# The MoE norm's gain moved from the rows into the experts' weight splits, and the second half's routing put ahead of weight splits on VectorE

## The chip, the cores and the metric

One core of one Trainium2 chip runs the kernel. The metric is the device time of one execution in microseconds (us). The core has five engines that work side by side: TensorE (PE, matmuls), VectorE (DVE), ScalarE (ACT), GpSimd (POOL) and SyncE (SP), of which the last issues most of the DMA transfers and POOL issues the gathers and scatters by index.

## The reference

One hybrid decoder layer on 1024 tokens of width 1024, in float32. Ahead of the part that is changed, a convolution branch, a forgetting attention and a cross-attention into 256 memory tokens are added to x. Then comes the mixture of experts, in two levels: the best of 4 groups, and of its 4 experts the best two.

```python
x = x + hierarchical_moe(rmsnorm(x, norm_moe_g[l]), ...)
return rmsnorm(x, norm_final_g)

def rmsnorm(x, g):
    y = xf * lax.rsqrt(jnp.mean(xf * xf, axis=-1, keepdims=True) + EPS)
    return y * g

def hierarchical_moe(h, wg, bg, we, be, w_gate, w_up, w_down):
    g_logits = hf @ wg + bg
    g_star = argmax(softmax(g_logits))
    e_sel = (hf @ we + be) of group g_star
    top_v, top_i = lax.top_k(softmax(e_sel), 2)
    weights = p_gsel[:, None] * top_v / sum(top_v)
    a = hf @ w_gate[e];  b = hf @ w_up[e]
    y = sum over e of (silu(a) * b * combine[e]) @ w_down[e]
```

Each of 16 experts has w_gate and w_up of 1024x256 and w_down of 256x1024.

## The kernel before

Every float32 product is made of three matmuls. An operand is split into a high part, rounded to the format that PE multiplies, and a low part, what is left of it: `split` writes the high part on ScalarE (line L134) and the low part on VectorE (L138) or GpSimd (L136). PE then multiplies high by high, low by high and high by low (L142 to L144). Weights come from memory as raw tiles (`w_raw` for the layers ahead, `e_raw` for gate and up, `d_raw` for down), 128x1024 at a time, and are split on the way. The split results are called `w_hi`, `w_lo`, `gu` and `dn`, and those of token rows `xgT`.

The tokens go through the end of the layer in two halves of 512 (four tiles of 128 rows). `xa_out(n)` adds the cross-attention of half n to x, makes the sums of squares and the router's raw products. `rows_of(hf)` turns the sums into the inverse root of the norm (n3v, n3t, n3r: some twelve small VectorE operations, with three Newton steps), scales the logits lg by it, writes the normed rows to memory (`h3_dram`), from which the experts' rows are gathered, and hands lg to the routing. The rows of the first half are scaled on ScalarE and multiplied by the gain `grow` on GpSimd (L926, tiles h3s); those of the second half are multiplied by the gain on GpSimd first, ahead of the norm (`gained`, L819, tiles hg), and scaled on ScalarE afterwards (L918). `grow` is the gain spread over all 128 partitions; the gain is also there as `g_moe`, eight columns with one number per partition, for use on transposed data.

`route_steps` finds the best group and the two best experts by masks (m, fm_s, fm_b, oh, ohg, E), counts tokens by matmuls (`M`, place in the queue of an expert, tm, q), builds selection matrices Am and B, and sums them on PE into slots (`slot_sums`, L1081). From these come `ids`, the list of token rows of each expert. It is a generator: its first piece runs to Am, and later pieces make the sums and ids.

`fetch` gathers rows xg by `ids` with a DMA that GpSimd issues (L1305). `turn` transposes them on PE (L1251, into the bank ps_tra) and splits them into xgT. `early_steps` and `early` multiply xgT with gate and up weights (ps_lin) and make uu, the activated product; `store` multiplies with the down weights and adds to the output by index. The first two experts' first-half rows are multiplied early, between the two routings, and fill PE while the second half is routed. Most experts' rows beyond 128 go in a second pass with fewer rows that uses the raw weights without splits (`gate_up_low`, `store_low`); for these `turn` copies the transposed rows with one ScalarE operation (L1316).

A scheduler orders each engine's instructions by the order in the code, which `tc.high_priority(offset)` moves ahead by so many places and `tc.issue_after` holds behind an instruction; the result is one fixed list for each engine, in which each instruction waits for its inputs.

Of the kernel before, what the change touches and what calls it, by code (L numbers as in the profile page):

```python
# [16 lines left out]
P = 128  # L17
D = 1024
T = 1024
KD = 8  # L20
# [35 lines left out]
def half(n):  # L56
    return slice(n * HALF, n * HALF + HALF)
# [7 lines left out]
def layer_kernel(ctx, tc, a, out, dbg=None):  # L65
# [700 lines left out]
    st, HG = {}, {}  # L766

    def xa_out(n):
# [19 lines left out]
        for m in range(KD):  # L788
# [5 lines left out]
            if m == 4:  # L794
                for k in range(4):
                    products(k)
                rows(0)
                if n:
                    HG[0] = gained(0)
# [10 lines left out]
        if n:  # L810
            HG[1] = gained(1)
        return ss

    def gained(b):

        tiles = [xt_p.tile([P, 2, HALF], F32, name=f"hg{b}", tag=("xt1a", "xt1b")[b], bufs=2) for _ in range(2)]
        hg = [x[:, i] for x in tiles for i in range(2)]
        for t in range(4):
            G.tensor_tensor(hg[t], x3[4 + t][:, half(b)], grow[:, half(b)], op=OP.mult)  # L819
        return hg  # L820
# [58 lines left out]
    grow = ro.tile([P, D], F32, name="grow", tag="grow", bufs=1)  # L879
    G.dma_start(grow, bcast_rows(a["moe_g_row"], D))  # L880
# [22 lines left out]
    def rows_of(hf, ss, htile=None):  # L903
# [10 lines left out]
        for i in range(H4):  # L914
            if hf:
                for b in range(2):
                    h = HG[b][i]
                    A.activation(h, h, AF.Copy, scale=r[:, i:i + 1])  # L918
                    nc.sync.dma_start(h3_dram[blk(t0 + i), half(b)], h)
                continue  # L920
            h = htile()
            if i in ():
                V.scalar_tensor_tensor(h, x3[t0 + i], r[:, i:i + 1], grow, op0=OP.mult, op1=OP.mult)
            else:
                A.activation(h, x3[t0 + i], AF.Copy, scale=r[:, i:i + 1])
                G.tensor_tensor(h, h, grow, op=OP.mult)  # L926
            nc.sync.dma_start(h3_dram[blk(t0 + i)], h)
# [266 lines left out]
    def gu_weights(src, tile_, raw_=raw_tile, parts=range(4), raws=None):  # L1194
        gu = [[], [], []]
        for b in parts:
# [6 lines left out]
            split(t[0], t[1], raw)  # L1203
# [24 lines left out]
    with pool("rows") as rw:  # L1228
# [7 lines left out]
        lg0 = rows_of(0, ss0, lambda: rw.tile([P, D], F32, name="h3s", tag="h3s", bufs=2))  # L1236
# [4 lines left out]
        with tc.high_priority(offset=600):  # L1241
            lg1 = rows_of(1, ss1)
# [65 lines left out]
    def turn(e, h):  # L1308
        if is_shared(e) and h == 1:
# [6 lines left out]
            A.activation(XT[e, h], pt, AF.Copy)  # L1316
# [123 lines left out]
    with tc.issue_after(order["mm"].ins):  # L1440
        next(route1)
# [69 lines left out]
    gfin = ro.tile([P, D], F32, name="gfin", tag="grow", bufs=1)  # L1511
# [212 lines left out]
```

## Time and profile before

| what | value |
|---|---|
| median of 3 runs | 1228.31 us (1223.48 to 1232.91) |
| the profiled execution | 1228.64 us |
| its span, first to last instruction | 1226.9 us |
| granted clock of PE, mean | 0.985 of full speed |
| PE busy | 1159.0 us, 94% |
| DVE, ACT, POOL busy | 843.0, 629.3, 404.5 us |

All times of rows count from the start of the span; the profiled execution is 1.7 us longer than its span. [...] A row of a timeline gives the start, the length, the engine, the line and operation, what is written and read, how many instructions of the kind follow one another, and in brackets how long the engine had been idle and what it waited for.

### The profile page before, as it was taken

The numbers are of one execution on the slowest core, as the hardware profiler recorded it, in microseconds if no ns is written. First come the engines' busy times: TensorE is split into PE (matmuls) and PEld (weight loads), VectorE is DVE, ScalarE is ACT, GpSimd is POOL, SyncE is SP. The second block draws the span as 40 slices with busy tenths as digits, with TensorE's granted clock in tenths as the row PEclk, the third lists the DMA queues.
The fourth block names the chain that finished last, engine by engine and source line by source line (L and its number), as shares of the span: only waits on it lengthen the run. The fifth ranks groups of instructions, "written<-read, shape, count | busy, mean of one in ns | idle before, by whom it ended". The sixth has DMA issues, their size and how long they took to land. (4 is left out here: it accounts for less than half of the span.)

```text
span 1226.9 us, 17120 instructions
## 1 busy us (share of the span) xinstructions
PE 1159.0 (94%) x6173; PEld 908.7 (74%) x6174; DVE 843.0 (69%) x1569; ACT 629.3 (51%) x1059; POOL 404.5 (33%) x276
## 2 busy tenths in 40 slices
PE   7999999999999999999999999999977898999995
PEld 3678887878877777788888788788754666667773
DVE  5499998653969787791235754755997784766665
ACT  6345664442646555471333342733742575767765
POOL 3327996221010100101012665273034133233433
PEclk9999999999999999999999999999998898999998
DMA  5211224136111111111343453144356889999967
GB/s 208 75 37 52 58 97 156 51 106 231 53 57 44 44 59 46 39 55 46 103 163 129 155 167 111 66 123 121 101 192 243 270 243 300 301 292 311 320 169 285
DMA packets 57467, 174.12 MB, mean 142 GB/s; under 512 B 7992, under 2 KB 11080, under 8 KB 57376
## 3 DMA queue, kind: packets, MB, share of 16 engines
q1 hardware_dynamic: 49680, 149.76, 36.5%
q0 software_dynamic: 7696, 23.20, 8.1%
q8 instruction: 51, 0.84, 0.3%
q14 instruction: 40, 0.33, 0.1%
HBM read 136.92 MB, written 36.01 MB: 141 GB/s over the span
## 5 line engine op out<-in xcount | busy, mean ns | idle before, releaser
L136 POOL TENSOR_TENSOR w_lo<-w_raw,w_hi 128x1024 fp32r<-128x1024 f32 x58 | 140.1, 2415 | 463.4 <-ACT w_hi L134 453.6
L144 PE MATMUL ps_lin<-hh,w_lo 128*128 128x512 f32 x560 | 221.4, 395 | 2.5 <-POOL w_lo L136 2.5
L142 PE MATMUL ps_lin<-hh,w_hi 128*128 128x512 f32 x560 | 223.0, 398 | 0.7 <-DVE u L357 0.6
L143 PE MATMUL ps_lin<-hl,w_hi 128*128 128x512 f32 x560 | 221.5, 396 | 0.0
L134 ACT ACTIVATE w_hi<-w_raw 128x1024 fp32r<-128x1024 f32 (+1 forms) x100 | 92.1, 921 | 201.0 <-PE ps_lin L143 169.1
L144 PEld LDWEIGHTS ps_lin<-hh,w_lo 128*128 128x128 f32 x560 | 105.3, 188 | 24.6 <-POOL w_lo L136 4.6
L142 PEld LDWEIGHTS ps_lin<-hh,w_hi 128*128 128x128 f32 x560 | 105.4, 188 | 23.3 <-issue 2.9
L143 PEld LDWEIGHTS ps_lin<-hl,w_hi 128*128 128x128 f32 x560 | 105.4, 188 | 21.5 <-issue 1.6
L379 DVE SCALAR_TENSOR_TENSOR ps_cva<-u,dw_w,ps_cva 128x1024 f32<-128x1024 f32 x90 | 111.6, 1280 | 0.5
L138 DVE SCALAR_TENSOR_TENSOR gu<-e_raw,gu 128x1024 fp32r<-128x1024 f32 x64 | 77.5, 1222 | 4.5 <-ACT gu L134 0.8
L375 POOL TENSOR_TENSOR oc<-oc,pj 128x512 f32<-128x512 f32 x60 | 75.8, 1303 | 8.8 <-ACT pj L374 8.7
L134 ACT ACTIVATE gu<-e_raw 128x1024 fp32r<-128x1024 f32 x64 | 67.4, 1058 | 8.0 <-PE ps_lin L144 7.4
L142 PE MATMUL ps_lin<-gu,xgT 128*128 128x512 f32 x144 | 58.8, 408 | 4.1 <-ACT xgT L134 4.1
L374 ACT ACTIVATE pj<-u,dw_w 128x512 f32<-128x512 f32 x60 | 42.4, 721 | 34.3 <-POOL oc L375 34.2
L138 DVE SCALAR_TENSOR_TENSOR dn<-d_raw,dn 128x1024 fp32r<-128x1024 f32 x32 | 39.0, 1225 | 27.8 <-ACT dn L134 24.0
L1305 POOL DMA_INDIRECT xg<-h_dram,ids x29 | 35.2, 1215 | 67.5 <-PE ps_sco L1081 24.3
L143 PE MATMUL ps_lin<-gu,xgT 128*128 128x512 f32 x144 | 57.4, 399 | 0.0
L560 ACT ACTIVATE sc<-sc,mns 128x128 f32<-128x128 f32 (+3 forms) x64 | 49.4, 772 | 15.6 <-DVE mns L556 15.0
L144 PE MATMUL ps_lin<-gu,xgT 128*128 128x512 f32 x144 | 57.0, 396 | 0.0
L138 DVE SCALAR_TENSOR_TENSOR pl<-ps_tra,ph 128x512 fp32r<-128x512 f32 (+1 forms) x80 | 49.1, 636 | 9.3 <-ACT ph L134 8.2
L134 ACT ACTIVATE ph<-ps_tra 128x512 fp32r<-128x512 f32 (+1 forms) x80 | 41.8, 552 | 23.3 <-PE ps_tra L573 22.5
L573 PE MATMUL ps_tra<-ident,sc 128*128 128x128 f32 x288 | 47.5, 274 | 4.1 <-DVE sc L563 4.1
(471 smaller groups left out, 2855.5 us busy)
## 6 DMA issues: line engine op xcount, KB each, us to landing
e_raw<-in_w_gu SPq DMA_DIRECT2D x64, 512.0 KB, 6.4
w_raw<-in_w_in SPq DMA_DIRECT2D x36, 512.0 KB, 3.7
d_raw<-in_w_dn SPq DMA_DIRECT2D x32, 512.0 KB, 9.6
w_raw<-in_w_out SPq DMA_DIRECT2D x16, 512.0 KB, 3.6
xT<-in_xT SPq DMA_DIRECT2D x16, 256.0 KB, 5.2
gc_dram<-gc SPq DMA_DIRECT2D x8, 512.0 KB, 4.0
gc<-gc_dram SPq DMA_DIRECT2D x8, 512.0 KB, 5.2
mc_dram<-gc SPq DMA_DIRECT2D x8, 512.0 KB, 2.8
```

The costliest lines, as they stand in the source:

```text
L134: order["split"] = A.activation(hi, src, AF.Copy, scale=scale)
L136: G.tensor_tensor(lo, src, hi.bitcast(F32), op=OP.subtract)
L138: V.scalar_tensor_tensor(lo, src, scale, hi.bitcast(F32), op0=OP.mult, op1=OP.subtract)
L142: TE.matmul(ps, lh, rh, start=first, stop=False)
L143: TE.matmul(ps, lh, rl, start=False, stop=False)
L144: return TE.matmul(ps, ll, rh, start=False, stop=last)
L374: A.activation(pj, uj, AF.Copy, scale=dw_h[:, c, j:j + 1])
L375: G.tensor_tensor(co[c][:, ns], co[c][:, ns], pj, op=OP.add)
L379: V.scalar_tensor_tensor(sums, u[c][:, j:j + T], dw_h[:, c, j:j + 1], sums, op0=OP.mult, op1=OP.add)
L560: A.activation(sc[:, :nk], sc[:, :nk], AF.Exp, scale=-1.0, bias=mns[:, nch - 1:nch], accum_out=sm)
L573: TE.transpose(pt[:, s_], pr[i][:, blk(j)], ident)
L1305: G.indirect_dma_start(out=XG[e, h][:n], out_offset=None, in_=src, in_offset=bass.IndirectOffsetOnAxis(ap=idx, axis=0))
```

## The change

The gain of the norm ahead of the experts is no longer multiplied into the rows. Gate and up weights take it in their split: each raw tile holds two blocks of 512 columns, and each block is split by itself with a scale of one number per partition, so the 64 tiles take 128 operations on ScalarE and 128 on VectorE where they took 64 and 64. The rows of the low-rank pass, which meet raw weights, take the gain in their copy, which moves from ScalarE to VectorE. All twelve GpSimd multiplications go, and with them the tile grow and its load. The second half's rows are scaled from x on ScalarE in four operations of 128x1024 and stored by four transfers, where there were eight of each. The first piece of the second routing gets a priority that puts it ahead of weight splits. The final gain, which lay in grow's place after its last use, has a place of its own and is loaded earlier.

```diff
@@ rows_of and its callers @@
-    grow = ro.tile([P, D], F32, name="grow", tag="grow", bufs=1)
-    G.dma_start(grow, bcast_rows(a["moe_g_row"], D))
...
-    def gained(b):
-
-        tiles = [xt_p.tile([P, 2, HALF], F32, name=f"hg{b}", tag=("xt1a", "xt1b")[b], bufs=2) for _ in range(2)]
-        hg = [x[:, i] for x in tiles for i in range(2)]
-        for t in range(4):
-            G.tensor_tensor(hg[t], x3[4 + t][:, half(b)], grow[:, half(b)], op=OP.mult)
-        return hg
...
         for i in range(H4):
-            if hf:
-                for b in range(2):
-                    h = HG[b][i]
-                    A.activation(h, h, AF.Copy, scale=r[:, i:i + 1])
-                    nc.sync.dma_start(h3_dram[blk(t0 + i), half(b)], h)
-                continue
-            h = htile()
...
-                A.activation(h, x3[t0 + i], AF.Copy, scale=r[:, i:i + 1])
-                G.tensor_tensor(h, h, grow, op=OP.mult)
+            h = htile(i)
+            A.activation(h, x3[t0 + i], AF.Copy, scale=r[:, i:i + 1])
             nc.sync.dma_start(h3_dram[blk(t0 + i)], h)
@@ gu_weights @@
-            split(t[0], t[1], raw)
+            for j in range(2):
+                split(t[0][:, j], t[1][:, j], raw[:, j], scale=g_moe[:, 2 * b + j:2 * b + j + 1])
@@ turn, low-rank rows @@
-            A.activation(XT[e, h], pt, AF.Copy)
+            V.tensor_tensor(XT[e, h], pt, g_moe[:, :, None].to_broadcast([P, KD, n]), op=OP.mult)
@@ after xa_out(1) @@
-            lg1 = rows_of(1, ss1)
+            lg1 = rows_of(1, ss1, lambda i: xt_p.tile([P, D], F32, name="h3t", tag=("xt1a", "xt1b")[i % 2], bufs=2))
...
     route1 = route_steps(1, lg1)
-    with tc.issue_after(order["mm"].ins):
+    with tc.issue_after(order["mm"].ins), tc.high_priority(offset=600):
         next(route1)
...
-    gfin = ro.tile([P, D], F32, name="gfin", tag="grow", bufs=1)
+    gfin = ro.tile([P, D], F32, name="gfin")
```

What this does to the engines' lists is seen at three places. The first is VectorE where the second half's norm is worked out; n3t and n3r are the Newton steps, xgT<-ps_tra the low halves of the early experts' rows. Before:

```order
L149 SCALAR_TENSOR_TENSOR n3t<-n3t,n3v 128x4
L150 SCALAR_TENSOR_TENSOR n3r<-n3t,n3r 128x4
L148 TENSOR_TENSOR n3t<-n3r 128x4
L149 SCALAR_TENSOR_TENSOR n3t<-n3t,n3v 128x4
L150 SCALAR_TENSOR_TENSOR n3r<-n3t,n3r 128x4
L910 TENSOR_TENSOR lg<-lg,n3r 128x80
L138 SCALAR_TENSOR_TENSOR xgT_8535<-ps_tra,xgT_8534 128x512
L911 TENSOR_TENSOR lg<-lg,rb 128x80
L953 TENSOR_REDUCE m_8614<-lg 128x16
```

After the change:

```order
L148 TENSOR_TENSOR n3t<-n3r 128x4
L149 SCALAR_TENSOR_TENSOR n3t<-n3t,n3v 128x4
L150 SCALAR_TENSOR_TENSOR n3r<-n3t,n3r 128x4
L138 SCALAR_TENSOR_TENSOR xgT_8525<-ps_tra,xgT_8524 128x512
L148 TENSOR_TENSOR n3t<-n3r 128x4
L138 SCALAR_TENSOR_TENSOR xgT_8525<-ps_tra,xgT_8524 128x512
L149 SCALAR_TENSOR_TENSOR n3t<-n3t,n3v 128x4
L150 SCALAR_TENSOR_TENSOR n3r<-n3t,n3r 128x4
L896 TENSOR_TENSOR lg<-lg,n3r 128x80
```

Now two low halves come in between the Newton steps where one came behind them all. On ScalarE the high halves moved likewise: three of the four stand ahead of the row scalings h3t, where one stood ahead of the eight hg.

The second place is VectorE from tm and q of the second half on (gu and dn are weight splits, Am the selection matrix, ssum the sums from which ids come). Before:

```order
L138 SCALAR_TENSOR_TENSOR gu_8577<-e_raw,gu_8576 128x1024
L138 SCALAR_TENSOR_TENSOR gu_8583<-e_raw,gu_8582 128x1024
L992 TENSOR_TENSOR tm_8674<-E,ps_sco 128x128
L993 TENSOR_REDUCE q_8675<-tm_8674 128x8
L997 TENSOR_SCALAR Am<-place,q_8675 128x256 x8
L1181 TENSOR_SCALAR over_9172<-q_8675 128x8
L1279 TENSOR_TENSOR uu<-uu,ps_lin 128x256
L138 SCALAR_TENSOR_TENSOR dn_8589<-d_raw,dn_8588 128x1024
L138 SCALAR_TENSOR_TENSOR dn_8595<-d_raw,dn_8594 128x1024
L138 SCALAR_TENSOR_TENSOR ul<-ps_acc,uh 128x256
L1084 TENSOR_REDUCE ssum<-ps_sco 128x32
```

After the change:

```order
L969 TENSOR_REDUCE q_8669<-tm_8668 128x8
L138 SCALAR_TENSOR_TENSOR xgT_8529<-ps_tra,xgT_8528 128x512
L138 SCALAR_TENSOR_TENSOR gu_8567<-e_raw,g_moe,gu_8566 128x512
L973 TENSOR_SCALAR Am<-place,q_8669 128x256 x8
L138 SCALAR_TENSOR_TENSOR gu_8567<-e_raw,g_moe,gu_8566 128x512
L138 SCALAR_TENSOR_TENSOR gu_8575<-e_raw,g_moe,gu_8574 128x512 x2
L1082 RECIPROCAL w_8849<-w_8849 128x4
L1157 TENSOR_SCALAR over_9174<-q_8669 128x8
L1256 TENSOR_TENSOR uu<-uu,ps_lin 128x256
L1060 TENSOR_REDUCE ssum<-ps_sco 128x32
L1083 TENSOR_TENSOR w_8849<-w_8849,pg 128x4
L984 TENSOR_TENSOR ssum<-ssum,idf_7404 128x32
```

Now tm (three rows ahead of the second fence) and q stand ahead of the gate/up splits, one half of a split stands ahead of Am, and the two down splits stand behind ssum and ids.

The third place is PE when the second half's first rows have been gathered (xg) and experts' early rows are stored (dn). Before:

```order
L1282 MATMUL ps_acc<-ident,uu 128x128 x2
L142 MATMUL ps_lin<-dn_8588,uh 128x512
L143 MATMUL ps_lin<-dn_8589,uh 128x512
L142 MATMUL ps_lin<-dn_8588,uh 128x512
L144 MATMUL ps_lin<-dn_8588,ul 128x512
L142 MATMUL ps_lin<-dn_8594,uh 128x512
L143 MATMUL ps_lin<-dn_8595,uh 128x512
L144 MATMUL ps_lin<-dn_8594,ul 128x512
L143 MATMUL ps_lin<-dn_8589,uh 128x512
L144 MATMUL ps_lin<-dn_8588,ul 128x512
L1251 MATMUL ps_tra<-ident,xg 128x128 x8
L142 MATMUL ps_lin<-dn_8594,uh 128x512
```

After the change:

```order
L1057 MATMUL ps_sco<-Bw,Am 128x48
L1228 MATMUL ps_tra<-ident,xg 128x128 x8
L1259 MATMUL ps_acc<-ident,uu 128x128 x2
L142 MATMUL ps_lin<-dn_8582,uh 128x512
L143 MATMUL ps_lin<-dn_8583,uh 128x512
L142 MATMUL ps_lin<-dn_8582,uh 128x512
L143 MATMUL ps_lin<-dn_8583,uh 128x512
L1228 MATMUL ps_tra<-ident,xg 128x128 x8
L144 MATMUL ps_lin<-dn_8582,ul 128x512
```

The transposes of the gathered rows stood behind nine matmuls with dn; now they stand ahead of the transposes of uu and of all of these.

## Rows read from the trace of the kernel before

**Rows 1.** Page, part 1: busy us, share of the span, instructions by engine.
```profile
PE 1159.0 (94%) x6173; PEld 908.7 (74%) x6174; DVE 843.0 (69%) x1569; ACT 629.3 (51%) x1059; POOL 404.5 (33%) x276
```

**Rows 2.** PE's waits from 900 to 985 us: total, times, longest.
```profile
PE ps_tra L1251 <- DVE xgT L138: 5.6, 1, 5.6
PE ps_lin L142 <- ACT xgT L134: 4.1, 1, 4.1
PE ps_st L1027 <- DVE w L1108: 3.8, 1, 3.8
PE ps_lin L144 <- DVE w_lo L138: 3.1, 1, 3.1
```

**Rows 3.** Stretches: length, busy per engine, granted clock, DMA share, GB/s.
```profile
920.00:930.00 10.00, 9.08 (x61) 4.90 (x61) 6.80 (x36) 0.84 (x2) 0.00 (x0) 0.66 0.26 86
950.00:960.00 10.00, 6.60 (x31) 5.20 (x32) 8.12 (x32) 7.32 (x12) 0.00 (x0) 0.54 0.89 313
1030.00:1040.00 10.00, 7.20 (x26) 6.17 (x27) 1.90 (x3) 3.71 (x7) 0.92 (x1) 0.66 1.03 334
1040.00:1100.00 60.00, 60.00 (x312) 42.17 (x312) 42.40 (x47) 44.00 (x63) 20.79 (x14) 1.00 0.99 308
```

**Rows 4.** Timeline of POOL: start, us, operation, count, idle before and releaser.
```profile
915.20 4.77 POOL L926 TENSOR_TENSOR h3s<-h3s,grow 128x1024 f32<-128x1024 f32 x2 [3.81 <-ACT h3s L925]
...
940.36 4.93 POOL L819 TENSOR_TENSOR hg<-x3r,grow 128x512 f32<-128x512 f32 x4 [2.18 <-ACT x3r L783]
969.61 0.97 POOL L1305 DMA_INDIRECT xg<-h_dram,ids  x1 [24.32 <-PE ps_sco L1081]
```

**Rows 5.** Timeline of DVE, the two routing halves.
```profile
909.08 2.33 DVE L958 TENSOR_TENSOR ohg<-fm_s,fm_b 128x16 f32<-128x16 f32 x1
...
915.35 2.40 DVE L982 TENSOR_SCALAR B<-E,toklo 128x128 bf16<-128x128 f32 x1
...
942.90 1.19 DVE L165 TENSOR_SCALAR n3v<-ssum 128x4 f32<-128x4 f32 x1
...
951.84 0.28 DVE L982 TENSOR_SCALAR B<-E,toklo 128x128 bf16<-128x128 f32 x1
```

**Rows 6.** Timelines of ACT, PE and DVE, second half, in order of time.
```profile
947.38 5.01 ACT L918 ACTIVATE hg<-hg,n3r 128x512 f32<-128x512 f32 x8 [4.55 <-DVE n3r L150]
...
953.40 0.79 PE L142 MATMUL ps_lin<-gu,xgT 128*128 128x512 f32 x1 [4.07 <-ACT xgT L134]
...
956.76 2.35 DVE L138 SCALAR_TENSOR_TENSOR gu<-e_raw,gu 128x1024 fp32r<-128x1024 f32 x2
959.94 0.29 DVE L992 TENSOR_TENSOR tm<-E,ps_sco 128x128 f32<-128x128 f32 x1 [0.82 <-PE ps_sco L989]
...
960.58 1.66 DVE L997 TENSOR_SCALAR Am<-place,q 128x256 bf16<-128x256 bf16 x8
...
964.12 1.23 DVE L138 SCALAR_TENSOR_TENSOR dn<-d_raw,dn 128x1024 fp32r<-128x1024 f32 x1 [0.47 <-ACT dn L134]
...
968.70 0.16 DVE L1009 TENSOR_SCALAR ids<-ssum 128x4 int32<-128x4 f32 x1
...
970.99 0.50 PE L142 MATMUL ps_lin<-dn,uh 128*128 128x512 f32 x1 [0.47 <-ACT uh L134]
...
974.73 1.09 PE L1251 MATMUL ps_tra<-ident,xg 128*128 128x128 f32 x8 [1.42 <-DMA xg<-h_dram,ids]
```

**Rows 7.** Groups (busy us, mean ns of one), and two source lines (ns min/median/max).
```profile
L138 DVE SCALAR_TENSOR_TENSOR gu<-e_raw,gu 128x1024 fp32r<-128x1024 f32 x64 | 77.5, 1222 | 4.5 <-ACT gu L134 0.8
...
L134 ACT ACTIVATE gu<-e_raw 128x1024 fp32r<-128x1024 f32 x64 | 67.4, 1058 | 8.0 <-PE ps_lin L144 7.4 <-DMA e_raw<-in_w_gu 0.2
...
L256 DVE SCALAR_TENSOR_TENSOR hl<-xT,g_mix,hh x16: 736/743/1555, 6.2 to 33.5; 128x512 fp32r<-128x512 f32 x16
...
L255 ACT ACTIVATE hh<-xT,g_mix x16: 705/707/722, 5.5 to 29.9; 128x512 fp32r<-128x512 f32 x16
```

**Rows 8.** PE's waits from 985 to 1200 us: total, times, longest.
```profile
PE ps_tra L1251 <- DMA xg<-h_dram,ids: 5.2, 2, 4.8
```

More of the change, by code (lines that the diff above doesn't have):

```diff
@@ L764, in xa_attend @@
             split(o2[n][0][h], o2[n][1][h], ps)
-    st, HG = {}, {}
+    st = {}
     def xa_out(n):
@@ L797, in xa_out @@
                 rows(0)
-                if n:
-                    HG[0] = gained(0)
         for k in range(4, KD):
@@ L809, in xa_out @@
         V.tensor_reduce(st[n], pt.rearrange("p t (g c) -> p t c g", g=4)[:, :, 0:20], axis=AX.X, op=OP.add)
-        if n:
-            HG[1] = gained(1)
-        return ss
-    def gained(b):
-        tiles = [xt_p.tile([P, 2, HALF], F32, name=f"hg{b}", tag=("xt1a", "xt1b")[b], bufs=2) for _ in range(2)]
-        hg = [x[:, i] for x in tiles for i in range(2)]
-        for t in range(4):
-            G.tensor_tensor(hg[t], x3[4 + t][:, half(b)], grow[:, half(b)], op=OP.mult)
-        return hg
+        return ss
     def row_tile(n):
@@ L901, in b4, with rows_of @@
         return x[:, :, None].to_broadcast([P, H4, n])
-    def rows_of(hf, ss, htile=None):
+    def rows_of(hf, ss, htile):
         t0 = H4 * hf
@@ L914, in rows_of @@
         for i in range(H4):
-            if hf:
-                for b in range(2):
-                    h = HG[b][i]
-                    A.activation(h, h, AF.Copy, scale=r[:, i:i + 1])
-                    nc.sync.dma_start(h3_dram[blk(t0 + i), half(b)], h)
-                continue
-            h = htile()
-            if i in ():
-                V.scalar_tensor_tensor(h, x3[t0 + i], r[:, i:i + 1], grow, op0=OP.mult, op1=OP.mult)
-            else:
-                A.activation(h, x3[t0 + i], AF.Copy, scale=r[:, i:i + 1])
-                G.tensor_tensor(h, h, grow, op=OP.mult)
+            h = htile(i)
+            A.activation(h, x3[t0 + i], AF.Copy, scale=r[:, i:i + 1])
             nc.sync.dma_start(h3_dram[blk(t0 + i)], h)
@@ L1234, in raw_rows @@
             return rw.tile([P, 2, HALF], F32, name="e_raw", tag="e_raw", bufs=2)
-        lg0 = rows_of(0, ss0, lambda: rw.tile([P, D], F32, name="h3s", tag="h3s", bufs=2))
+        lg0 = rows_of(0, ss0, lambda i: rw.tile([P, D], F32, name="h3s", tag="h3s", bufs=2))
         backs = [weights(0, *route(0, lg0))]
```

## The prediction

> **What bounds the kernel now.** The busy shares come first: TensorE (PE) works 1159.0 of 1226.9 us, VectorE (DVE) 843.0, ScalarE (ACT) 629.3, GpSimd (POOL) 404.5 [rows 1]. The kernel is PE's list of matmuls, and a change pays only where PE stands still or runs at its low clock. PE's waits inside 900 to 985 us say where that is in the part that the change touches: 3.1 us for a low weight half w_lo, 3.8 for the routing of the first token half, 5.6 and 4.1 for xgT, the transposed rows of the first experts [rows 2]. The stretches by ten microseconds add the price behind a wait: granted clock 0.66 in 920 to 930 and 0.54 in 950 to 960, while the expert loop from 1040 on has PE busy 60 of 60 us at clock 1.00, DVE 42.4, ACT 44.0 and a DMA share of 0.99 [rows 3]. So there are two soft spots, one for each routing half, and then a loop in which only PE counts.
>
> Both spots have GpSimd in them. Its multiplications by the gain run as two of 4.77 us in all at 915.20 and as four of 4.93 us in all at 940.36 [rows 4]. VectorE's small steps beside them stretch and end where GpSimd's operation ends: an operation on 128x16 takes 2.33 us from 909.08, one on 128x128 takes 2.40 from 915.35, where the same line of the second half, with GpSimd idle, takes 0.28; a step on 128x4 takes 1.19 at 942.90, and the next one as long again [rows 5]. The waits for w_lo and for the routing end on VectorE just behind those stretches.
>
> **First half: what goes.** The change takes GpSimd's multiplications out altogether. Without them the stretched steps go back to about 0.2 to 0.3 us each, so VectorE gets back 2.1 us ahead of w_lo (2.33 less 0.2) and 2.1 ahead of the routing's count (2.40 less 0.28) by these two rows alone, and each has a neighbour stretched by nearly as much. The waits that they feed are 3.1 and 3.8 us [rows 2]: I let both go, 6.9 us. The clock in 920 to 930 is 0.66 [rows 3]: at half speed for a share x of the ten microseconds, 1 - x/2 = 0.66, so 6.8 us at the low level, in which 3.4 us of full-speed work were lost. The fall follows right behind the two waits; with them gone I count the 3.4 us back as well. Sum 10.3 us, which is a ceiling.
>
> **First half: what comes.** Six weight tiles of the first experts are split here, each now as two 128x512 operations with a gain per partition in place of one 128x1024 with a constant. The nearest rows with such a scale are in the first stage of the kernel: on VectorE 736 to 743 ns (minimum and median), on ScalarE 707 [rows 7]. A pair on VectorE is then 1.49 us against 1.22, 0.27 more; on ScalarE 1.41 against 1.06, 0.35 more by the medians, or 0.25 if the pair runs as closely packed as the eight 128x512 operations that take 5.01 us at 947.38 [rows 6]: 2 x 0.626 = 1.25 against 1.00. Six tiles, by the count of the order, cost VectorE 1.6 us, and the last pair now stands inside the first half's Newton steps (the inverse root of the row norm), so it lies on the path of the routing. I take 1.5 us off: **8.8 us** from this half, between 4 (only one of the two waits goes, and the clock falls anyway) and 10.3.
>
> **Second half.** Before, the two stretched steps at 942.90 last until GpSimd is done at 945.3; then come the rest of the Newton steps, and only then the first low half of xgT, which frees PE's bank. On ScalarE the eight scalings of rows (hg, 5.01 us from 947.38) stand ahead of the other xgT splits. So PE's first expert matmul is at 953.40 [rows 6]. In the changed order three xgT splits stand ahead of the row scalings (now four of 128x1024) and two of VectorE's low halves go into the Newton steps. Worked out: 942.3 for the first step, ten steps of about 0.2 us up to the second Newton round, 944.3; two low halves of about 0.7 (a little under the 0.74 of [rows 7], which has a scale to read), 945.7; eight transposes of 1.1 us (as the last of [rows 6]), and the first matmul is at about 946.8, 6.6 us earlier.
>
> What ends last after that is the list of token numbers, ids, at 968.70, which lets GpSimd gather the second half's rows at 969.61; they land 5.1 us later, at PE's transposes of 974.73 [rows 4, 6]. The chain up to it: tm at 959.94 (it waits for small matmuls that PE reaches only after its first expert matmuls, at half clock), Am from 960.58 for 1.66 us, then PE's sums and ids, with two splits of down weights (1.23 us each, the first at 964.12) ahead of the reduction on VectorE, and two splits of gate/up weights (2.35 us at 956.76) ahead of tm [rows 6]. The changed order sets tm and q ahead of the gate/up splits, one half split ahead of Am, and the down splits behind ids; in exchange three xgT halves (2.1 us) now lie inside the chain ahead of the masks. The masks before would be done about 2.6 us earlier for the missing stretch and 2.1 later for the halves, so about 951.1 against 951.64; PE's small matmuls come at about 952, tm at 952.4, q 0.6 later, one xgT half and one gate/up half (1.4), Am done at 956.1. From the end of Am (960.58 plus 1.66, 962.24) to ids were 6.5 us, in which the down splits held the reduction back by about one of them; without that 5.2, so ids at 961.3, the gather 0.9 later at 962.2 or a little before, landing 5.1 us later at about 967: 7.7 us earlier than 974.73. In the changed order PE's transposes wait there **ahead of** nine matmuls of the down projection which stood ahead of them before: they ran from 970.99 to 973.31 (974.73 less the idle 1.42 ahead of it), 2.3 us [rows 6], which no longer fill the wait. Net, with the 0.47 that PE waited ahead of them given back, **5.9 us**; if the clock gate and the order are kinder, 8; if the gather lands as late as in the loaded stretch, 3 us less.
>
> **The sum.** 1228.64 (the profiled execution) - 8.8 - 5.9 = 1213.9; it lies 0.33 us above the median of 1228.31, so I forecast 1213.5 for the median. The low-rank rows' turn, from a ScalarE copy to a VectorE multiplication by the gain, ten times, costs nothing in a loop where VectorE has 17.6 of 60 us free [rows 3]; if it were on the path, ten times about 0.1 us. The final gain's own buffer takes one broadcast load out of the stretch in which the second half's rows are gathered and puts it ahead, among the cross-attention's loads; I count it at nothing, between 0 and 1 us gained, since no wait of PE there names it.
>
> **The loop, where the change costs.** All but the first six of the 64 tiles are split later than that, most of them in the loop. ScalarE's 44.0 and VectorE's 42.4 of 60 us [rows 3] rise by four tiles an expert of about 13 us: 1.0 to 1.4 us on ScalarE (8.1 to 8.4 of 10), 1.1 on VectorE (7.9 of 10). Neither fills up, and PE waits for no split there now, so I take 0 and keep 64 x (0.25 to 0.35) = 16 to 22 us of ScalarE and 64 x 0.27 = 17 us of VectorE as the price should the cover go.
>
> [...]
>
> **Rivals.** (1) *The entry into the loop gives the second gain back.* From 1040 on the DMA share is 0.99 [rows 3], and the largest later wait of PE is a gather: 4.8 of 5.2 us [rows 8], followed by a stretch at clock 0.66 [rows 3]. If weights or gathers cannot come earlier, the second half's 5.9 us turn into a longer wait there: 1213.5 + 5.9 = 1219.4. For it: the share; against: PE waits for no weight load in the loop. (2) *That later stall goes too.* Its 4.8 us and 3.4 us of lost clock hang on a gather that lands late; should the shifted order let it land in time, 1213.5 - 8 = 1205.5. Nothing in the order aims at it. (3) *The splits become the loop's bound, and the kernel is slower.* ScalarE and VectorE work on one tile in turn, and the pair adds to both: 64 x (0.25 + 0.27) = 33 us with nothing hidden, half of that with ScalarE's share hidden, 17; from 1213.5 that gives 1230 to 1247, and I take 1238. It decides where PE begins to wait for gu in the loop, that is where a tile's turn on the slower engine exceeds PE's time for it, six matmuls or 1.5 us at the 2.3 us of nine above: VectorE's pair of 1.49 is at that mark, ScalarE's of 1.25 to 1.41 under it; against it stands that tiles are split an expert ahead. (4) *The change does not do what it moves:* GpSimd's work was not what held the first half, and another late input (the w_lo's own load) holds PE there: 1213.5 + 8.8 = 1222, and with (1) 1228.
>
> **Chances.** Forecast 1213.5, with its own range 1208 to 1219: 0.54. Rival 1, 1219.4: 0.18. Rival 2, 1205.5: 0.11. Rival 3, 1238: 0.07. Rival 4, 1222 to 1228: 0.10. The runs of before spread over 1223 to 1233, so a measurement of this kernel can tell 1% from no change, 12.3 us: faster is below 1216.0, slower above 1240.6. Of the forecast's own case about 0.7 lies below 1216 (0.38), all of rival 2 (0.11) and a quarter of rival 1 (0.05): 0.54 faster. Slower is a part of rival 3, 0.04. Same is the rest, 0.42. Leaving out rival 3 and the far end of 4, and a little below rival 2, the range is 1203 to 1225.
>
> **What would show it.** In the profile after: no GpSimd multiplication near 906 to 945, mask and weight steps of 0.15 to 0.3 us on VectorE throughout; PE's waits for w_lo and for w gone and the clock 1.00 where it was 0.66; hg replaced by four ScalarE operations behind three xgT splits; ids about 17 us earlier on the clock of the span; PE's transposes waiting for the gather some 5 us with the down matmuls behind them; in the loop gu pairs of 1.25 to 1.4 us on ScalarE and 1.4 to 1.5 on VectorE with PE busy throughout. I am wrong if PE waits for gu in the loop, if the clock falls after the earlier first matmul, or if the wait for w_lo stays though VectorE is free.

## The result and the profile after

The changed kernel takes 1218.20 us at the median of twelve runs (1217.19 to 1225.35), the kernel before 1228.44 (1220.97 to 1232.91): a ratio of 0.9924, 95% interval 0.9907 to 0.9942. That is 10.2 us less by the medians and 0.76% less by the ratio, inside the range that was given and 4.7 us above the time that was forecast; by the mark of 1% it is "within 1%", which had a chance of 0.42. A second comparison (experiment e9) gave 0.9959. The profiled execution took 1219.29 us with a span of 1217.5.

Part 1 of the page after, against [rows 1]: GpSimd lost 23.6 us, ScalarE gained 13.9, PE's work is the same.

```profile
PE 1160.9 (95%) x6173; PEld 910.3 (75%) x6174; DVE 841.9 (69%) x1643; ACT 643.2 (53%) x1109; POOL 380.9 (31%) x263
```

PE's waits of the kernel after, from 800 to 985 us: total, times, longest.

```profile
PE ps_tra L1228 <- DVE xgT L138: 3.4, 1, 3.4
PE ps_tra L1228 <- DMA xg<-h_dram,ids: 3.4, 1, 3.4
PE ps_acc L707 <- POOL oacc L698: 2.4, 1, 2.4
PE ps_sco L781 <- DVE ss L784: 0.6, 1, 0.6
```

The waits for w_lo and for the first half's routing w [rows 2] are gone, and that of 4.1 us for ScalarE's xgT as well. The other xgT wait is 3.4 us, where the kernel before had 5.6; e4 below, which has the lists of before up to that place, had 3.2, so this difference can't be put down to the change. Two are larger: the gather's, foreseen, and one for oacc, the sum of squares, 70 us ahead of the place where anything was expected (0.6 before).

Stretches of the kernel after, columns as in [rows 3].

```profile
820.00:840.00 20.00, 17.59 (x69) 14.32 (x68) 12.04 (x45) 4.40 (x6) 12.28 (x24) 0.84 0.58 166
920.00:930.00 10.00, 10.00 (x74) 5.80 (x75) 7.06 (x32) 1.72 (x3) 2.03 (x2) 1.00 0.47 159
940.00:950.00 10.00, 6.40 (x37) 5.16 (x38) 8.78 (x51) 6.17 (x10) 0.00 (x0) 0.83 0.87 342
960.00:970.00 10.00, 6.88 (x26) 5.70 (x27) 7.32 (x20) 3.73 (x6) 1.88 (x2) 0.66 0.81 274
1030.00:1090.00 60.00, 60.00 (x312) 42.47 (x311) 45.23 (x66) 47.92 (x77) 19.26 (x14) 1.00 1.01 319
```

920 to 930 is full at clock 1.00, where it was 0.66. In the loop PE is busy 60 of 60 us beside a ScalarE with 47.9 (44.0 before) and a VectorE with 45.2 (42.4). In the second half the clock is 0.83 in 940 to 950, where 950 to 960 had 0.54. The low clock has come up at two other places: 0.84 around the oacc wait and 0.66 behind the gather's.

VectorE's timeline after, the lines of [rows 5].

```profile
912.65 0.17 DVE L934 TENSOR_TENSOR ohg<-fm_s,fm_b 128x16 f32<-128x16 f32 x1
...
916.75 0.28 DVE L958 TENSOR_SCALAR B<-E,toklo 128x128 bf16<-128x128 f32 x1
...
940.56 0.17 DVE L165 TENSOR_SCALAR n3v<-ssum 128x4 f32<-128x4 f32 x1
```

2.33, 2.40 and 1.19 us have become 0.17, 0.28 and 0.17. The second half in the timelines of ACT, PE, DVE and POOL after, in order of time, against [rows 6].

```profile
939.22 1.08 ACT L134 ACTIVATE xgT<-ps_tra 128x512 fp32r<-128x512 f32 x2
942.98 1.97 PE L1228 MATMUL ps_tra<-ident,xg 128*128 128x128 f32 x8 [3.42 <-DVE xgT L138]
944.63 4.26 ACT L902 ACTIVATE h3t<-x3r,n3r 128x1024 f32<-128x1024 f32 x4
944.78 0.80 PE L142 MATMUL ps_lin<-gu,xgT 128*128 128x512 f32 x1
951.36 1.66 DVE L973 TENSOR_SCALAR Am<-place,q 128x256 bf16<-128x256 bf16 x8
956.02 0.17 DVE L985 TENSOR_SCALAR ids<-ssum 128x4 int32<-128x4 f32 x1
956.93 0.95 POOL L1282 DMA_INDIRECT xg<-h_dram,ids  x1 [26.98 <-DVE Bw L1101]
962.59 1.41 PE L1228 MATMUL ps_tra<-ident,xg 128*128 128x128 f32 x8 [3.39 <-DMA xg<-h_dram,ids]
```

The row scalings (h3t) stand behind three xgT splits, PE's first expert matmul starts at 944.78 (953.40 before), ids at 956.02 (968.70), and PE's transposes wait for the gather until 962.59 (974.73).

**Where the time went.** Two operations of each half mark the way on the span's clock: the reduction lg, with which the routing begins, and ids, with which it ends. Their starts on VectorE cut the span into five stretches, in us:

| kernel | to lg, half 0 | to ids, half 0 | to lg, half 1 | to ids, half 1 | to the end |
|---|---|---|---|---|---|
| before | 900.3 | 25.3 | 16.2 | 27.0 | 258.2 |
| changed | 904.2 | 18.3 | 17.4 | 16.1 | 261.5 |
| difference | +3.9 | -7.0 | +1.2 | -10.9 | +3.3 |
| PE idle, before | 28.7 | 7.2 | 1.3 | 9.7 | 21.1 |
| PE idle, changed | 31.0 | 0.0 | 1.2 | 3.6 | 20.8 |

The sum of the differences is -9.4 (they are rounded one by one), the difference of the two spans. The two routings are 17.9 us shorter, and the stretches around them about half as much longer. Shorter and longer stretches are not yet gain and loss, since the marks stand on VectorE and PE goes on through its own list between them; PE's idle time tells the two apart. It is 13.3 us less inside the routings and 2.3 more ahead of them, 11.3 less in all, while PE's busy time rose by 1.9. Behind ids the stretch is 3.3 us longer with no more idle time: there PE has 3.6 us more work left when ids are ready. The stretch from ids to the end, columns as in [rows 3], before and then after:

```profile
968.70:1226.90 258.20, 237.13 (x1567) 171.53 (x1566) 170.66 (x284) 169.45 (x259) 89.64 (x58) 0.97 0.90 278
956.02:1217.50 261.48, 240.72 (x1583) 175.03 (x1581) 186.51 (x361) 183.56 (x308) 85.51 (x58) 0.97 0.90 279
```

### The profile page after: what moved, and what is told of

Read it like the earlier page. It is cut to its first block, busy times and chain, and to the rows that moved or that the text cites. A ratio compares the mean times of both kernels' runs of the same rounds, so it can differ in the third digit from the quotient of the medians.

```text
span 1217.5 us, 17220 instructions
## 1 busy us (share of the span) xinstructions
PE 1160.9 (95%) x6173; PEld 910.3 (75%) x6174; DVE 841.9 (69%) x1643; ACT 643.2 (53%) x1109; POOL 380.9 (31%) x263
## 4 chain that ended last, share of the span: by engine, by line
PE 68%; DVE 9%; POOL 8%; DMA 6%; ACT 6%; issue 3%; SPq 0%; ACTq 0%; DVEq 0%; POOLq 0%
PE ps_lin L142 16%; PE ps_lin L143 16%; PE ps_lin L144 16%; POOL oc L375 5%; PE ps_acc L589 3%; PE ps_tra L573 2%; DMA xg<-h_dram,ids 2%; POOL w_lo L136 2%; PE ps_sco L1347 2%; PE ps_tra L1228 2%; DMA at<-attn_dram 2%; PE ps_sco L551 1%; PE ps_sco L552 1%; PE ps_sco L1364 1%; DMA xo_dram<-yt,sids 1%
## 5 line engine op out<-in xcount | busy, mean ns | idle before, releaser
L138 DVE SCALAR_TENSOR_TENSOR gu<-e_raw,g_moe,gu 128x512 fp32r<-128x512 f32 x128 | 89.9, 747 | 0.3 <-ACT gu L134 0.2
L134 ACT ACTIVATE gu<-e_raw,g_moe 128x512 fp32r<-128x512 f32 x128 | 84.8, 718 | 5.0 <-PE ps_lin L144 3.6
L142 PE MATMUL ps_lin<-mgh,w_hi 128*128 128x512 f32 x128 | 50.1, 392 | 0.9 <-DVE ga L640 0.9
## 6 DMA issues: line engine op xcount, KB each, us to landing
d_raw<-in_w_dn SPq DMA_DIRECT2D x32, 512.0 KB, 10.2
```

Of the source, the lines that this page charges most:

```text
L134: order["split"] = A.activation(hi, src, AF.Copy, scale=scale)
L138: V.scalar_tensor_tensor(lo, src, scale, hi.bitcast(F32), op0=OP.mult, op1=OP.subtract)
L142: TE.matmul(ps, lh, rh, start=first, stop=False)
```

## The experiments

The same stretches for all runs, worked out from their traces in the same way, with each median of runs, and the ratio to the kernel before on the same chip:

| run | to lg 0 | to ids 0 | to lg 1 | to ids 1 | to end | median us | ratio, 95% |
|---|---|---|---|---|---|---|---|
| e1 | 902.9 | 18.3 | 17.4 | 16.1 | 260.3 | 1219.56 | 0.9930 (0.9904 to 0.9956) |
| e2 | 902.6 | 25.0 | 17.5 | 27.7 | 261.9 | 1236.51 | 1.0057 (1.0036 to 1.0079) |
| e3 | 902.6 | 18.3 | 17.4 | 16.0 | 265.9 | 1220.49 | 0.9932 (0.9907 to 0.9958) |
| e4 | 901.6 | 23.8 | 14.7 | 26.7 | 259.2 | 1228.12 | 0.9996 (0.9968 to 1.0025) |
| e5 | 904.3 | 18.3 | 15.7 | 15.9 | 262.2 | 1219.21 | 0.9953 (0.9924 to 0.9982) |
| e6 | 903.8 | 17.0 | 13.8 | 23.9 | 261.6 | 1220.38 | 0.9948 (0.9928 to 0.9967) |
| e7 | 902.5 | 18.3 | 15.7 | 15.7 | 265.7 | 1214.64 | 0.9899 (0.9877 to 0.9921) |
| e8 | 901.4 | 18.3 | 15.8 | 15.7 | 262.0 | 1215.43 | 0.9910 (0.9881 to 0.9940) |
| e9 | 904.7 | 18.3 | 17.4 | 16.6 | 264.8 | 1222.27 | 0.9959 (0.9934 to 0.9983) |
| e10 | 907.9 | 18.3 | 15.7 | 16.7 | 259.1 | 1219.71 | 0.9935 (0.9912 to 0.9957) |
| e11 | 903.2 | 24.1 | 17.4 | 15.7 | 263.3 | 1225.93 | 0.9988 (0.9964 to 1.0011) |
| e12 | 901.6 | 18.3 | 15.7 | 15.8 | 261.6 | 1215.58 | 0.9891 (0.9853 to 0.9928) |

The middle three stretches repeat within 0.5 us for the changed kernel and e9, and for e7 and e12, which are equal kernels. In the order of before they don't: up to 950 us e4's lists are those of the kernel before, and it needs 38.5 us from the first lg to the second where that needs 41.4. PE waited 2.7 us for w in e4 and 3.8 before. The last stretch doesn't repeat either: e7 and e12 differ by 4.1 us there, the changed kernel and e9 by 3.3. A single profile therefore says little about the tail, and the medians are needed for it.

**e1: only the load of the gain rows is kept.** The change took a broadcast load out of GpSimd's list. The rows of POOL and PE before, and then after, show what that did.

```profile
829.54 0.57 POOL L880 DMA_DIRECT2D grow<-in_moe_g_row  x1
831.25 1.28 POOL L698 TENSOR_TENSOR oacc<-oacc,osq 128x512 f32<-128x512 f32 x1 [1.13 <-ACT osq L697]
832.58 1.05 PE L707 MATMUL ps_acc<-ones,oacc 128*128 128x1 f32 x8 [0.59 <-POOL oacc L698]
832.68 2.36 POOL L136 TENSOR_TENSOR w_lo<-w_raw,w_hi 128x1024 fp32r<-128x1024 f32 x1
```

```profile
829.29 2.40 POOL L136 TENSOR_TENSOR w_lo<-w_raw,w_hi 128x1024 fp32r<-128x1024 f32 x1 [0.25 <-ACT w_hi L134]
831.64 1.71 POOL L698 TENSOR_TENSOR oacc<-oacc,osq 128x512 f32<-128x512 f32 x1
833.41 1.79 PE L707 MATMUL ps_acc<-ones,oacc 128*128 128x1 f32 x8 [2.41 <-POOL oacc L698]
```

Without the load the scheduler puts a weight half of 2.40 us ahead of the last addition of squares, and PE, which needs that sum, stands still 2.41 us.

```diff
+    grow = ro.tile([P, D], F32, name="grow", tag="grow", bufs=1)
+    G.dma_start(grow, bcast_rows(a["moe_g_row"], D))
...
-    gfin = ro.tile([P, D], F32, name="gfin")
+    gfin = ro.tile([P, D], F32, name="gfin", tag="grow", bufs=1)
```

> The changed kernel, with the load of grow kept (nothing reads it) and the final gain back in its place behind it. On GpSimd this puts the last addition of the squares (oacc, L698) ahead of the next w_lo again, as before the change. My theory: the changed kernel lost 4 to 5 us near 830 us, because that addition fell behind a 2.4 us w_lo, PE waited 2.4 us for it and then ran at half clock; so this run is 4 to 5 us faster than the changed kernel, about 1213.5, with no PE wait over 1 us at L707 and granted clock 1.00 in 820 to 840. Rival: the loss is made up later by other waits, and the time stays at 1218.

The old order came back, the wait is 0.6 us and the clock in 820 to 840 is 1.00. A mark just ahead of that place, VectorE's last row addition x2T of L691, tells what this is worth. From its start to lg of half 0 it is 71.2 us in the kernel before, 75.9 in the changed kernel, 76.2 in e9 and 71.3 in e1, so e1 has the 4 to 5 us back there. e3, with the same wait of 2.41 us but the clock at 1.00, needs 72.9. So the wait by itself costs 1.7 us, and the low clock, where it follows, 3 more.

On the span's clock lg comes only 1.3 us earlier in e1 than in the changed kernel, for e1 ran at 0.91 in 240 to 260 and in 330 to 350, where the changed kernel had 1.00. The expected 4 to 5 us don't show in the median either: 1219.56 can't be told from that of the changed kernel. The mechanism is shown in the traces; as a gain by itself it isn't shown.

**e2: GpSimd busy again.** On top of e1, twelve multiplications without use on GpSimd, of the shapes that the change removed and where they stood; they add work and leave nothing out.

```diff
+            if not hf:
+                G.tensor_tensor(grow, h, h, op=OP.mult)
...
+    def gained(b):
+        for t in range(4):
+            G.tensor_tensor(grow[:, half(b)], x3[4 + t][:, half(b)], x3[4 + t][:, half(b)], op=OP.mult)
```

> The kernel of e1 (grow's load kept) with twelve GpSimd multiplications put back at the old places, of the old shapes (four of 128x1024 on the rows h3s, eight of 128x512 on x), writing into grow, which nothing reads; the second half's rows do not depend on them. Theory that GpSimd's operations cost by stretching VectorE's steps beside them: VectorE's steps of the routing take 1 to 2.4 us again and the run loses 5 to 8 us against e1. Rival, that what cost was the dependence of the stored rows on GpSimd: same time as e1 within 1.5 us, though steps may be stretched.

1236.51 us: 17 us above e1, more than twice the 5 to 8 that were expected, and 0.57% above the kernel before. Both routings are as long as before (25.0 and 27.7 us). The timelines of POOL, DVE and PE in e2, in order of time:

```profile
909.95 3.87 POOL L915 TENSOR_TENSOR grow<-h3s 128x1024 f32<-128x1024 f32 x2 [62.77 <-ACT h3s L913]
910.00 0.68 DVE L793 TENSOR_TENSOR x2T<-ps_lin,x2T 128x512 f32<-128x512 f32 x1
910.84 1.08 DVE L947 TENSOR_TENSOR oh<-fm_s,fm_b 128x64 f32<-128x64 f32 x1
912.02 1.88 DVE L957 SCALAR_TENSOR_TENSOR es<-oh,lg 128x64 f32<-128x64 f32 x1
...
942.33 1.04 POOL L817 TENSOR_TENSOR grow<-x3r 128x512 f32<-128x512 f32 x1 [10.54 <-ACT x3r L783]
943.53 1.05 POOL L1295 DMA_INDIRECT xg<-h_dram,ids  x1 [0.16 <-issue]
950.71 1.97 PE L1241 MATMUL ps_tra<-ident,xg 128*128 128x128 f32 x8 [6.95 <-DMA xg<-h_dram,ids]
```

Two things are to be seen. oh and es (0.22 and 0.21 us in the changed kernel) take 1.08 and 1.88 us and end where the two GpSimd operations end, at 911.9 and 913.8, while x2T, which is longer and takes one operand from the bank ps_lin, has its usual 0.68 beside the same operation. Why the one kind of step stretches and the other doesn't is not shown. The second thing was not in the prediction: the gather of half 0 stands behind a multiplication in GpSimd's own list. ids of half 0 was ready at 927.6, the gather goes out at 943.53, and PE stands still 6.95 us for its rows. The kernel before had this queue too, with its ids at 925.5 and the gather behind four multiplications:

```profile
930.16 5.52 POOL L819 TENSOR_TENSOR hg<-x3r,grow 128x512 f32<-128x512 f32 x4 [10.20 <-ACT w_hi L134]
935.85 1.05 POOL L1305 DMA_INDIRECT xg<-h_dram,ids  x1 [0.17 <-issue]
```

In e2 it stands behind a fifth as well, which waited 10.54 us for its input. So e2 has GpSimd's work of before, but not its exact order, and its 17 us can't be taken as the price of that work in the kernel before. In the changed kernel the gather goes out at 927.62, 5 us behind its ids.

**e11: only the first half's four multiplications** (e2 without `gained`).

> The kernel of e1 with only the first half's four GpSimd multiplications put back (results unused). It splits e2's loss. By my prediction the first half's GpSimd work is worth 6.9 to 10.3 us: 7 to 10 us slower than e1's 0.993, so about 1.000 of the kernel before, with PE waits of 3 to 4 us for w_lo or w. If most of e2's loss was the gathers queued on GpSimd behind the second half's multiplications: within 3 us of e1.

VectorE's steps are stretched as in e2 and PE waits for w_lo again. Two rows of DVE and one of PE's waits from 800 to 985 us, of e11:

```profile
911.45 1.08 DVE L943 TENSOR_TENSOR oh<-fm_s,fm_b 128x64 f32<-128x64 f32 x1
912.62 1.88 DVE L953 SCALAR_TENSOR_TENSOR es<-oh,lg 128x64 f32<-128x64 f32 x1
PE ps_lin L144 <- DVE w_lo L138: 3.7, 1, 3.7
```

1225.93 us; against e1 the first routing is 5.8 us longer, the second as in e1, and the ratios differ by 0.58%, about 7 us, where each of the two ratios is known to 3 us or so. So the first half's GpSimd work costs some 6 to 7 us, and the rest of e2, 8.5 us by the ratios and 10.6 by the medians, is the second half's, with the gather that it holds up: its routing takes 27.7 us against 15.7.

**e3 and e4: the priority of the routing.** e3 is the changed kernel without it, e4 the kernel before with it.

```diff
-    with tc.issue_after(order["mm"].ins), tc.high_priority(offset=600):
+    with tc.issue_after(order["mm"].ins):
```

> The changed kernel without the priority of the second routing's first piece. VectorE then does four gate/up halves ahead of q, and Am waits for them. If that priority is what brings ids early: ids about 1.4 to 3 us later than in the changed kernel and the time up by as much, 1220 to 1221. If the gather's rows are not what ends last there, the time stays at 1218.

> The kernel before with the priority of the second routing's first piece alone. The order of VectorE changes by little (tm still stands behind two whole gate/up splits), so I expect no difference from the kernel before: 1228, within 2 us. If the priority were the larger part of the change, 1222 or less.

The second routing takes 16.0 us without the priority and 16.1 with it; in the kernel before it takes 26.7 with it and 27.0 without. The times agree: e3 has a ratio of 0.9932, the changed kernel 0.9924 and 0.9959, and e4 0.9996. The priority is worth nothing that can be measured here.

**e6: whole tiles again.** The gate and up weights are split as 128x1024 with a constant, as before; the gain is left out of these weights.

```diff
-            for j in range(2):
-                split(t[0][:, j], t[1][:, j], raw[:, j], scale=g_moe[:, 2 * b + j:2 * b + j + 1])
+            split(t[0], t[1], raw)
```

> The changed kernel with whole 128x1024 splits of the gate and up weights by a constant; the gain is left out of these weights, so the experts' result lacks it. It prices the split into halves. By my prediction the halves cost nothing in the loop and about 1.5 us ahead of the first routing: 1216 to 1217. Rival, the halves cost in the loop too (ScalarE and VectorE busier by 8 to 11%): 1210 or less, with the tail from ids to the end shorter by 5 us or more.

The whole is not faster (1220.38), and PE is busy 60 of 60 us in the loop here too: the halves cost the loop nothing. Around the routings they matter in both directions. From lg of half 0 to lg of half 1 e6 needs 30.7 us, the changed kernel 35.7: there the halves cost 5.0, though I had priced them at 1.5. The second routing needs 23.9 against 16.1: there they save 7.8. Timelines of ACT and PE in e6 show one reason:

```profile
937.53 4.27 ACT L902 ACTIVATE h3t<-x3r,n3r 128x1024 f32<-128x1024 f32 x4 [3.20 <-DVE n3r L150]
941.90 1.05 ACT L134 ACTIVATE xgT<-ps_tra 128x512 fp32r<-128x512 f32 x2
943.01 0.79 PE L142 MATMUL ps_lin<-gu,xgT 128*128 128x512 f32 x1 [3.75 <-ACT xgT L134]
```

With whole tiles the scheduler sets the row scalings ahead of xgT again, as before the change [rows 6], and PE waits for xgT. The order with three xgT splits ahead comes from the halves, not from the priority. It isn't the only thing that e6 puts back: on VectorE two whole gate/up splits (2.36 us) stand ahead of tm again and two down splits (2.36 us) ahead of ids. The 7.8 us are those of all three orders together, with the clock that goes with them (0.74 in 930 to 950, 0.91 in the changed kernel); no run separates them.

**e5: the router's products together.** Of the 5.0 us 1.3 lie between lg and ids of half 0; of the rest PE's own list has a large part. The eight products of the second half's router, 32 columns each, stand on PE of the changed kernel as follows (two records make a product):

```profile
918.94 1.05 PE L775 MATMUL ps_st<-x2T,wr 128*32 128x512 f32 x2
...
920.14 1.06 PE L775 MATMUL ps_st<-x2T,wr 128*32 128x512 f32 x6
...
925.22 1.04 PE L775 MATMUL ps_st<-x2T,wr 128*32 128x512 f32 x2
...
927.43 1.04 PE L775 MATMUL ps_st<-x2T,wr 128*32 128x512 f32 x2
...
933.46 1.05 PE L775 MATMUL ps_st<-x2T,wr 128*32 128x512 f32 x2
...
935.02 1.04 PE L775 MATMUL ps_st<-x2T,wr 128*32 128x512 f32 x2
```

and in e6:

```profile
920.34 1.07 PE L775 MATMUL ps_st<-x2T,wr 128*32 128x512 f32 x8
...
928.59 1.90 PE L775 MATMUL ps_st<-x2T,wr 128*32 128x512 f32 x8
```

Four in a row take 1.07 us, one alone 1.04 to 1.05. Pulled apart into six groups the eight take 6.3 us, in e6 3.0, in the kernel before 3.8 with the first four at half clock (1.94 us from 925.16, granted clock 0.50). Three more behind the first cost 0.02 to 0.03 us. e5 makes each product of the second half wait for the last of its four inputs:

```diff
+            if n:
+                tc.add_manual_dep(i.ins, order["x2", m | 3].ins.name, ...)
```

> The changed kernel in which the second half's router products (L775, 32 columns wide, four of them side by side in PE) wait until four can run together, as they stood before the change; in the changed kernel they stand in six groups of 1, 3, 1, 1, 1, 1 and each group takes about 1.05 us, whether it holds one or four. Theory that this is where part of the first half's gain went: three groups fewer, 3.1 us of PE's time, so the logits of the second half and ids come 3 us earlier against the first half's, and the kernel about 3 us faster than the changed one: 1215. Rival, that the second half is bound by VectorE or by transfers: within 1 us of 1218.

They take 3.2 us in all, the stretch between the routings is 1.7 us shorter, less than the 3.1 saved, since PE now waits 1.3 us for the row additions. The 3 us that were expected of the median don't show (0.9953).

**e7: with that, the last addition of squares on VectorE**, out of GpSimd's list.

```diff
-                G.tensor_tensor(acc, acc, sq, op=OP.add)
+                (V if n and m == 7 else G).tensor_tensor(acc, acc, sq, op=OP.add)
```

> The kernel of e5 with the last addition of squares (oacc) on VectorE in place of GpSimd, so that no 2.4 us w_lo stands ahead of it. If both losses add up: e5's time less 2 to 4 us, about 1212, with PE's wait at L707 under 0.6 us. If the 2.4 us are made up later, as e1 hints: the same as e5 within 1.5 us.

0.9899 from four runs, and ids of half 1 at 952.2 (956.0 in the changed kernel). PE's wait for the sum is 1.5 us, not under 0.6 as expected.

**e8: with both, PE's transposes of the second half's rows behind the down matmuls**, which fill the wait for the gather.

```diff
+    order["dn0"] = order["dn"]
...
-    with tc.high_priority(offset=100):
+    with tc.issue_after(order["dn0"].ins):
```

> The kernel of e7 with the transposes of the second half's first gathered rows put behind the down matmuls of the first half (store of expert 0), the order before the change. My prediction priced the changed order at 2.3 us: PE waits for the gather with these matmuls behind the wait. If right: 2 us faster than e7, more if the clock then does not fall in 960 to 970. Rival: the down matmuls are not ready then either, since their weight splits and uh now come late, and the time stays at e7's within 1 us.

The wait for the gather, 2.7 us in e7, is gone and the clock in 960 to 970 is 1.00 (0.77 in e7); a wait of 1.8 us for uu has come instead, and the median (1215.43) is that of e7. This gain is not shown.

**e9 and e10: the changed kernel again, and all three repairs**, with the sum of squares left on GpSimd and the weight half held behind it.

> The changed kernel itself, on the same chip and beside the same runs of the kernel before as the next two, for a direct comparison: 0.992 of the kernel before, as measured first.

> The changed kernel with three repairs of order: the last addition of squares ahead of the next w_lo on GpSimd (by holding that w_lo behind it), the router products of the second half four together, and the transposes of the second half's first gathered rows behind the down matmuls. If the order's side effects are what held the gain back: 0.985 to 0.990 of the kernel before and 3 to 8 us faster than the changed kernel. If the loop's entry gives back whatever comes earlier (stalls on gathers near 1020): 0.991 to 0.993, the same as the changed kernel, with ids earlier by 4 to 6 us and the tail from ids to the end longer by as much.

e10 missed: 0.9935. The hold made the weight half late in turn: PE waits 1.8 us for oacc and 0.8 for w_lo, 2.6 in all where e9 has 2.4, so this repair repaired nothing. From the row addition that was used as a mark in e1 to lg of half 0 it is 76.9 us (76.2 in e9). lg comes 3 us later than in e9, but 2.5 of these were lost ahead of that mark, where e10 ran at 0.91 in 240 to 260 and in 330 to 350 and e9 at 1.00; they are not the hold's. Why the other two repairs don't show in the median is open.

**e12: e7 once more.**

> The kernel of e7 once more (the second half's router products behind the fourth row addition, and the last addition of squares on VectorE), to see whether its 0.9899 stands. Theory (the two side effects of the change cost some 3 us of the median): ratio to the kernel before 0.987 to 0.9915. Rival (e7 was the low end of the scatter, and what is saved ahead of ids is lost later): 0.992 to 0.996, as the changed kernel measured in its two comparisons (0.9924 and 0.9959). In both cases the profile has PE's wait for oacc at 1.5 us in place of 2.4 and ids near 952.

0.9891, beside 0.9899 the first time. PE's waits in e12 from 800 to 985 us:

```profile
PE ps_tra L1230 <- DMA xg<-h_dram,ids: 4.0, 1, 4.0
PE ps_tra L1230 <- DVE xgT L138: 3.4, 1, 3.4
PE ps_acc L707 <- DVE oacc L698: 1.4, 1, 1.4
```

Both medians, 1214.64 and 1215.58, lie below both of the changed kernel, 1218.20 and 1222.27, by some 5 us on average. By the ratios it is 3 to 8 us, and the intervals still overlap with that of the first comparison, so the size is not settled. It is the best version measured, 1.0 to 1.1% under the kernel before.

## Why the prediction was right, and where its sizes were off

**GpSimd beside VectorE: shown as a cause.** e2 gives all of the gain back and more (a ratio of 1.0057 where e1 has 0.9930), e11 the first half's part alone (0.9988), in both with results that nothing reads. Rival 4 (GpSimd not what held the first half) is out.

**First half, 8.8 us forecast.** From lg of half 0 to lg of half 1 the changed kernel is 5.7 us shorter (7.0 less 1.2). Against e4, the second execution in the old order, it is 2.7 shorter, so 5.7 is the upper end. The two waits and the low clock went as foreseen: PE's idle time from lg to ids fell from 7.2 us to nothing, and the clock in 920 to 930 rose from 0.66 to 1.00. The half speed with which the prediction worked out the 3.4 us is in the trace of before: a granted clock of 0.50 in 922 to 924. e6, without the halves, is 10.7 shorter than before (41.4 to 30.7) and 7.8 shorter than e4; the ceiling of 10.3 fits the first of these only. The step that failed is the price of what comes, 1.5 us, which measured 5.0: 1.3 on VectorE's path (18.3 against 17.0 to ids), near the forecast, and the rest on PE, where the order that the scheduler makes with halves pulls the router's products apart, 6.3 us of work for 3.0. e5, which puts them together, gets 1.7 of these 3.7 us back; the other 2 are open. I had read the order around the expert splits alone, not PE's rows between them.

**Ahead of both halves, nothing forecast.** lg of half 0 comes 3.9 us later. The step was "I count it at nothing", for the broadcast load that leaves GpSimd's list. A load that nobody waited for had kept two operations in an order that PE liked. From the last row addition to lg, the mark used in e1, the loss is 4.7 us: about 1.8 are the longer wait, and the clock of 0.84 over 20 us accounts for the other 3. The changed kernel had come to that mark 0.8 us earlier than the kernel before. What the low clock costs ahead of lg is not the change's alone: e1, e3 and e10 ran at 0.91 in 240 to 260, and so did e4, which has the lists of before up to 950 us and lg 1.3 us later.

**Second half, 7.4 us up to ids forecast, measured 10.9.** The 7.4 are 968.7 less 961.3; the 7.7 of the prediction is for the landing of the gather, and by its own terms (962.2 and 5.1) that is 7.4 as well. The first matmul came 8.6 us earlier on the span and 6.9 earlier against lg (6.6 forecast), and the masks followed. But the reason given was incomplete. The orders that come with the halves are worth 7.8 of it (e6), and they need a free GpSimd, or the gathers of half 0 come late (e2): that queue was not in the prediction. The named part of the change, the precedence of the routing, does nothing that shows (e3, e4).

**Behind ids, 1.8 us back forecast (2.3 less 0.47), measured 3.3** in this profile. PE's transposes start 6.6 us behind ids, 6.0 before, and the nine down matmuls stand behind them, as foreseen; the low clock there (0.66 in 960 to 970) was one of the signs of being wrong that the prediction named. Over the whole tail the eight executions whose ids come before 958 are 2.1 to 7.7 us longer than the 258.2 of before, 4.8 on average, about 3 more than forecast. Rival 1 explained such a loss by longer waits at the entry into the loop. The profile doesn't bear it out: PE is idle 20.8 us behind ids and was 21.1 before, and the DMA share is 0.90 in both; what grew is PE's work that was still to do, 237.1 to 240.7 us. Beyond the nine down matmuls the prediction left out that PE is not as far in its list when ids come sooner. Between equal kernels the tail differs by idle time for the most part: 20.8 and 23.9 us in the changed kernel and e9, 21.6 and 24.5 in e12 and e7.

**Rivals 2 and 3 are out.** PE's later wait for a gather is 4.0 us where it was 4.8 [rows 8], so that stall did not go. Where two stand alone in the loop's timeline (from 1036 us) the pair takes ScalarE 1.33 us (1.25 to 1.41 forecast) and VectorE 1.42 (1.49), and PE waits for no gu. Groups of the kernel after: busy, mean of one.

```profile
L138 DVE SCALAR_TENSOR_TENSOR gu<-e_raw,g_moe,gu 128x512 fp32r<-128x512 f32 x128 | 89.9, 747 | 0.3 <-ACT gu L134 0.2
...
L134 ACT ACTIVATE gu<-e_raw,g_moe 128x512 fp32r<-128x512 f32 x128 | 84.8, 718 | 5.0 <-PE ps_lin L144 3.6 <-DMA e_raw<-in_w_gu 0.8
```

ScalarE's 17.4 us more than before (84.8 less the 67.4 of [rows 7]) and VectorE's 12.4 lie beside PE's work.

In sum, the forecast had -14.7 us on the span: the routings brought -16.6 from the first lg to the second ids (16.2 forecast by its terms, 16.5 in its sum), but 3.9 were lost ahead and 1.5 more than forecast behind. That the two halves together came out so near is luck: the first brought 3.1 less than forecast and the second 3.5 more, each for reasons that were not in the prediction. ids are 12.7 us earlier on the span, not 17.

## What to carry to other kernels

Work on an idle engine is not free where steps of others stretch beside it, or where what others wait for stands behind it in its list: here VectorE's small steps took 1.19 to 2.40 us beside GpSimd's operations in the kernel before and 0.17 to 0.28 without them in the changed one, and in e2 GpSimd issued its gather at 943.53 with ids ready at 927.6. That is worth looking for first where steps of 0.2 us take 1 to 2. When an edit takes instructions out or changes their shape, compare the order of every engine over the whole program, not only around the edit: the two costs that were missed were an addition that fell behind a weight half, 70 us ahead, and small matmuls that were pulled apart on PE. And try each named part of a change by itself: one of the two named here had no effect that could be measured. Before a late mark is put down to an edit, look how late the execution already was ahead of the edit: e10 and e1 had each lost some 2.5 us or more at a low clock (0.91 in 240 to 260 and in 330 to 350) long before the place that was changed.

## What was not expected of the hardware

One 32-column product costs PE what four in a row cost, 1.04 us (changed kernel) beside 1.07 (e6). The granted clock after a wait of the same 2.41 us, at the same place, was 0.84, 0.83 and 1.00 over 820 to 840 in three executions (the changed kernel, e9, e3); why is open. e3 alone of these had already been at 0.91 in 240 to 260, and no run tells whether the two hang together.
